# The 16 meta tokens last in a head's output step, and their rows turned by a 16-column product

## The chip, the cores and the metric

One core of a Trainium2 chip runs the whole program. The metric is the time of one execution in microseconds (us). Lower is better. TensorE (PE) does the matrix products, VectorE (DVE) and ScalarE (ACT) the elementwise work and the reading of PSUM, GpSimd (POOL) a few small operations, and SyncE (SP) issues the loads.

## The reference, cut to what matters

Two layers work on 528 tokens: 16 learned meta tokens, prepended, and 512 tokens of input. Each layer has eight heads, four of retention and four of gated linear attention (GLA). A head's output goes through a normalisation over its 128 values and is multiplied with a gate; the eight heads together go through one output projection.

```python
def _head_group_norm(o, w):           # retention heads
    mu = jnp.mean(o, axis=-1, keepdims=True)
    var = jnp.mean(jnp.square(o - mu), axis=-1, keepdims=True)
    y = (o - mu) * lax.rsqrt(var + EPS)
...
def _head_rms_norm(o, w):             # GLA heads
    y = o * lax.rsqrt(jnp.mean(o * o, axis=-1, keepdims=True) + EPS)
...
    o_ret = _head_group_norm(o_ret, ret_norm_w) * jax.nn.silu(rg.astype(jnp.float32))
    o_gla = _head_rms_norm(o_gla, gla_norm_w) * jax.nn.silu(gr.astype(jnp.float32))
    merged = jnp.concatenate([o_ret, o_gla], axis=-1).astype(h.dtype)
    return merged @ w_out
```

The rest of a layer is the input projection (`h @ w_in`, 3600 columns), and a gated MLP with a short convolution.

## The kernel before, in words

Activations lie transposed: features on partitions, the 528 tokens along the free dimension, cut into two column ranges (`SPLIT` at 232). Weights come as float32, and are split into a high and a low float16 part (L122 on ACT, L126 on DVE); each product of a weight tile is three float16 matmuls (L472 to L474). `mixer` walks over the tiles of the input projection (PSUM tile `pj`), and after each it calls `advance`, which takes steps of generators that work on the heads whose inputs are there. After the last tile, `drain` runs what is left of them, and `out_proj` (PSUM tile `po`) follows.

For the heads the tokens are cut differently, in `HEADS`: piece 0 is the 16 meta tokens, pieces 1 to 4 are 128 tokens each. `head_out` is the step at the end of a head. A call takes one retention head or two GLA heads, so a layer has six calls for its eight heads.

- Products. Per head, pieces 1 to 4 go into one PSUM bank `o`, piece 0 into another, `o2`, of which 16 rows are used. L777 makes `o2`, L779 the inner part of the four pieces, L783 adds the part from the state. A float32 product appears as two matmuls in the trace.
- Statistics. For a retention head, L794 and L795 on DVE, per piece; L403 on DVE and a power on POOL (L406) give the reciprocal roots of all five pieces at once. For GLA heads, squares with a sum on ACT (L801), then L405 on DVE and L406.
- Scaling. Each piece is scaled into an SBUF tile: by L806 on DVE (retention) or L808 on ACT (GLA). Pieces 1 to 4 go into `on`, piece 0 into `ont`, a slot of a shared room (the trace calls it `room`) whose unused rows were zeroed.
- A pause of two steps and a wait for the gate; then the turn. L819 transposes each piece back to features on partitions, into PSUM tiles `pto`: one for pieces 0, 1, 2 (272 columns), one for pieces 3, 4 (256 columns). The transpose of piece 0 writes 128 columns, of which those behind the first 16 are written again by piece 1. L822 on DVE multiplies a finished `pto` with norm weight and gate, L410 (ACT) and L411 (DVE) split it to float16 in `merged`.

The list `each` sets the order of the pieces in statistics and scaling: piece 0 first.

PSUM tiles come from two pools: `pmm` with three banks for the large products, `pmx` with five for all else, `o`, `o2` and `pto` among them.

The order in which the instructions stand in each engine's queue is the one of the Python program only up to the ninth weight tile of the first layer (`manual_schedule`). From there on a planner orders each engine's queue when the program is built: it takes the work in the order written, but lets later work pass what by its own reckoning is not ready. On the chip the queues are then fixed: an instruction that waits holds up all behind it on its engine.

Of the kernel before, what the change touches and what calls it, by code (L numbers as in the profile page):

```python
# [14 lines left out]
P = 128  # L15
NMETA = 16
SEQ = 512
L = NMETA + SEQ
# [11 lines left out]
HEADS = [(0, NMETA)] + [(NMETA + P * i, P) for i in range(4)]  # L30
MID = HEADS[3][0]
# [187 lines left out]
class Kern:  # L219
# [547 lines left out]
    def head_out(self, heads):  # L767

        nc = self.nc
        n = len(heads)
        os = [self.mx([P, 4, P], "o") for _ in heads]
        o2s = [self.mx([P, P], "o2") for _ in heads]
        for (intra, _, _, vn, *_), o, o2 in zip(heads, os, o2s):
            nc.tensor.matmul(o2, intra(0), vn(0), start=True, stop=True)  # L777
            for i in range(4):
                nc.tensor.matmul(o[:, i, :], intra(i + 1), vn(i + 1), start=i == 0, stop=i == 0, skip_group_check=i > 0)  # L779
        for i in range(4):  # L780
            c0 = HEADS[i + 1][0]
            for (_, qT, sn, *_), o in zip(heads, os):
                nc.tensor.matmul(o[:, i, :], qT[:, c0 : c0 + P], sn[:, i, :], start=False, stop=True, skip_group_check=True)  # L783
        src = lambda h, i: os[h][:, i - 1, :] if i else o2s[h][:NMETA]
        ret = heads[0][-1] is not None
        onvs = [(self.g([P, 4, P], F32, "on"), self.sm([P, P], "ont")) for _ in heads]
        to = lambda h, i: onvs[h][0][:, i - 1, :] if i else onvs[h][1][:NMETA]
        each = [(h, i, HEADS[i][1]) for h in range(n) for i in range(5)]
        if ret:
            mv = self.sm([P, 5, 2], "mv")  # L790
            nc.gpsimd.memset(mv[:, 0, :], 1.0)
            for h, i, wi in each:
                st = self.sm([P, 6], "bst")
                nc.vector.bn_stats(out=st[:wi], in_=src(h, i))  # L794
                nc.vector.bn_aggr(out=mv[:wi, i, :], in_=st[:wi])  # L795
            r = self.rstd(mv[:, :, 1], 5, 1.0, self.decay[:, 1, heads[0][-1], :])
        else:
            q = self.sm([P, n, 5], "ms")
            nc.gpsimd.memset(q[:, :, 0], 1.0)
            for h, i, wi in each:  # L800
                nc.scalar.activation(to(h, i), src(h, i), AF.Square, accum_out=q[:wi, h, i : i + 1])  # L801
            r = self.rstd(q.rearrange("p h i -> p (h i)"), 5 * n, 1.0 / P, EPS * 64.0)
        for h, i, wi in each:
            rr = r[:wi, 5 * h + i : 5 * h + i + 1]
            if ret:
                nc.vector.tensor_scalar(out=to(h, i), in0=src(h, i), scalar1=mv[:wi, i, 0:1], scalar2=rr, op0=ALU.subtract, op1=ALU.mult)  # L806
            else:
                nc.scalar.activation(to(h, i), src(h, i), AF.Copy, scale=rr)  # L808
        yield
        yield from self.pause(2)  # L810
        for (on, ont), (*_, wcol, gate, slot, _) in zip(onvs, heads):
            while gate[0] is None:
                yield "waits"
            merged = self.merged[slot] = self.g([P, 2, L], F16, "merged")
            for t0, t1, n0, n1 in [(0, 3, 0, MID), (3, 5, MID, L)]:
                pt = self.mx([P, WN], "pto")
                for t in range(t0, t1):
                    c0 = HEADS[t][0] - n0
                    nc.tensor.transpose(pt[:, c0 : c0 + P], on[:, t - 1, :] if t else ont, self.ident)  # L819
                t = self.sm([P, WN], "tmp")  # L820
                w = n1 - n0
                nc.vector.scalar_tensor_tensor(out=t[:, :w], in0=pt[:, :w], scalar=self.par[:, wcol : wcol + 1], in1=gate[0][:, n0:n1],  # L822
                                               op0=ALU.mult, op1=ALU.mult)
                self.split(merged, t[:, :w], n0, n1)
            yield
# [673 lines left out]
```

## Time and profile before

| | before |
|---|---|
| runs | 1238.57 us median of 3 (1238.42 to 1238.85) |
| the profiled execution | 1238.61 us; first to last instruction 1236.8 us |
| granted TensorE clock | 0.997 |
| PE / weight loads / DVE / ACT / POOL busy | 1214.2 / 1015.2 / 871.4 / 676.8 / 162.9 us |
| chain of work that ended last | PE 80%, DVE 10%, ACT 4% |

The "busy" time of an engine counts each instruction from its start to its end, and matmuls overlap; so the distance from one matmul's start to the next start tells more than their durations. In the timeline a row is start, duration, engine, line, operation, tiles out<-in, shape and count, and in brackets the idle time before it with what ended it.

### The profile page before, as it was taken

The page shows a single profiled execution, that of the slowest core. Times are in us where ns is not written, and L with a number is a line of the kernel's source. Part 1 is how long each engine was busy: PE and PEld are TensorE (multiplying, and loading weights), DVE is VectorE, ACT ScalarE, POOL GpSimd, SP SyncE. Part 2 cuts the span into 40 slices and gives each one's busy share as a digit, 9 for nine tenths or more (in the row PEclk, how much of TensorE's full clock was granted, in tenths as well). Part 3 has the DMA queues.
Part 4 walks back from the last instruction along what each step waited for, and adds up shares of the span by engine and source line. Part 5 has one row for each costly group of instructions (what it writes and reads, how often), then busy time and mean ns, then how long its engine had stood idle before and what let it go on. Part 6 is the DMA issues. An engine that isn't in the chain of part 4 may idle for free.

```text
span 1236.8 us, 26441 instructions
## 1 busy us (share of the span) xinstructions
PE 1214.2 (98%) x11031; PEld 1015.2 (82%) x11031; DVE 871.4 (70%) x1541; ACT 676.8 (55%) x1337; POOL 162.9 (13%) x211
## 2 busy tenths in 40 slices
PE   9999999999999999999999999999999999999997
PEld 8778889888788888888887788898798888886444
DVE  5677845367998889623465878443779998887686
ACT  5675444454776666523335754454637776664452
POOL 2012311153000000000230123011520000000001
PEclk9999999999999999999999999999999999999999
DMA  7932221131422423424232332221303363304471
GB/s 199 277 103 86 67 73 52 52 92 46 131 75 69 120 87 108 141 80 102 69 105 68 104 87 70 71 68 52 103 19 103 96 178 104 120 1 171 147 253 68
DMA packets 207259, 124.17 MB, mean 100 GB/s; under 512 B 6992, under 2 KB 194692, under 8 KB 207140
## 3 DMA queue, kind: packets, MB, share of 16 engines
q1 hardware_dynamic: 206836, 121.83, 33.8%
q8 instruction: 86, 1.41, 0.5%
q0 software_dynamic: 160, 0.52, 0.1%
q14 instruction: 33, 0.27, 0.1%
q10 hardware_dynamic: 144, 0.13, 0.0%
HBM read 120.37 MB, written 2.10 MB: 99 GB/s over the span
## 4 chain that ended last, share of the span: by engine, by line
PE 80%; DVE 10%; ACT 4%; issue 3%; POOL 2%; DMA 1%; SPq 0%; POOLq 0%; DVEq 0%; ACTq 0%
PE pl L1340 8%; PE pu L473 8%; PE pu L474 8%; PE pu L472 8%; PE pj L472 7%; PE pj L474 6%; PE pj L473 6%; PE pp L1159 5%; PE pd L472 3%; PE pd L473 3%; PE pd L474 3%; PE po L472 2%; PE po L474 2%; PE po L473 2%; DVE unit L126 2%
## 5 line engine op out<-in xcount | busy, mean ns | idle before, releaser
L473 PE MATMUL pu<-every,unit 128*128 128x296 f16 (+2 forms) x1120 | 306.1, 274 | 2.6 <-DVE every L411 2.6
L474 PE MATMUL pu<-every,unit 128*128 128x296 f16 (+2 forms) x1120 | 306.1, 274 | 0.0
L472 PE MATMUL pu<-every,unit 128*128 128x296 f16 (+2 forms) x1120 | 304.5, 274 | 0.7 <-ACT every L410 0.7
L474 PEld LDWEIGHTS <-unit 128*128 128x128 f16 x2572 | 252.0, 98 | 42.1 <-issue 3.4
L472 PEld LDWEIGHTS <-unit 128*128 128x128 f16 x2572 | 252.2, 98 | 41.1 <-issue 3.1
L473 PEld LDWEIGHTS <-unit 128*128 128x128 f16 x2572 | 252.4, 98 | 39.6 <-issue 2.9
L126 DVE SCALAR_TENSOR_TENSOR unit<-st,unit 128x1024 f16<-128x1024 f32 (+1 forms) x165 | 202.1, 1228 | 78.9 <-ACT unit L122 78.3
L472 PE MATMUL pj<-every,unit 128*128 128x296 f16 (+2 forms) x888 | 244.9, 276 | 3.0 <-ACT gv L1013 1.6
L474 PE MATMUL pj<-every,unit 128*128 128x296 f16 (+2 forms) x888 | 244.7, 276 | 0.9 <-DVE unit L126 0.9
L473 PE MATMUL pj<-every,unit 128*128 128x296 f16 (+2 forms) x888 | 244.9, 276 | 0.0
L122 ACT ACTIVATE unit<-st 128x1024 f16<-128x1024 f32 x163 | 169.7, 1042 | 79.2 <-PE pd L474 22.8
L438 DVE TENSOR_TENSOR acc<-acc,sq 128x296 f32<-128x296 f32 (+2 forms) x60 | 33.3, 556 | 73.9 <-ACT sq L436 72.1
L1159 PEld LDWEIGHTS <-unit 128*128 128x128 f16 x756 | 73.9, 98 | 13.3 <-issue 2.3
L474 PE MATMUL pd<-av,unit 128*128 128x232 f16 (+1 forms) x308 | 84.7, 276 | 0.0
L473 PE MATMUL pd<-av,unit 128*128 128x232 f16 (+1 forms) x308 | 84.7, 276 | 0.0
L472 PE MATMUL pd<-av,unit 128*128 128x296 f16 (+1 forms) x308 | 84.5, 276 | 0.0
L1215 ACT ACTIVATE u<-pu 128x296 f32<-128x296 f32 (+2 forms) x140 | 52.5, 378 | 50.2 <-PE pu L474 49.2
L406 POOL TENSOR_TENSOR every<-every 128x5 f32<-128x5 f32 (+6 forms) x31 | 38.1, 1231 | 293.5 <-DVE every L405 253.3
L1340 PE MATMUL pl<-unit,fk 128*128 128x512 f16 x330 | 71.4, 379 | 0.0
L474 PE MATMUL po<-merged,unit 128*128 128x296 f16 (+2 forms) x256 | 69.6, 274 | 0.0
L473 PE MATMUL po<-merged,unit 128*128 128x296 f16 (+2 forms) x256 | 69.6, 274 | 0.0
L1204 DVE SCALAR_TENSOR_TENSOR cg<-u,every,cg 128x527 f32<-128x527 f32 (+1 forms) x88 | 66.2, 752 | 4.7 <-ACT cg L1199 4.3
(272 smaller groups left out, 1908.6 us busy)
## 6 DMA issues: line engine op xcount, KB each, us to landing
st<-in_ffn_up SPq DMA_DIRECT2D x70, 512.0 KB, 4.0
st<-in_w_in SPq DMA_DIRECT2D x56, 512.0 KB, 4.4
st<-in_ffn_down SPq DMA_DIRECT2D x46, 512.0 KB, 4.4
st<-in_ffn_up SPq DMA_DIRECT2D x36, 256.0 KB, 3.8
st<-in_w_out SPq DMA_DIRECT2D x16, 512.0 KB, 4.2
st<-in_ffn_down SPq DMA_DIRECT2D x8, 384.0 KB, 3.6
out<-yo SPq DMA_DIRECT2D x7, 256.0 KB, 2.1
xt<-in_x SPq DMA_DIRECT2D x6, 256.0 KB, 6.3
```

What stands on the lines that cost most here:

```text
L122: self.kern.nc.scalar.activation(self.u[:, 0], self.st, AF.Copy, scale=SW)
L126: self.kern.nc.vector.scalar_tensor_tensor(out=self.u[:, 1, ks], in0=self.st[:, ks], scalar=SW, in1=self.u[:, 0, ks], op0=ALU.mult, op1=AL ...
L406: nc.gpsimd.tensor_tensor(out=r[:w, :n], in0=t[:w, :n], in1=self.mhalf[:w, :n], op=ALU.pow)
L438: eng.tensor_tensor(out=acc[:, :n], in0=acc[:, :n], in1=sq[:, :n], op=ALU.add)
L472: nc.tensor.matmul(ps[:, :n], w[:, 0, kk, :], x[:, 0, n0:n1], start=first, stop=False)
L473: nc.tensor.matmul(ps[:, :n], w[:, 0, kk, :], x[:, 1, n0:n1], start=False, stop=False)
L474: nc.tensor.matmul(ps[:, :n], w[:, 1, kk, :], x[:, 0, n0:n1], start=False, stop=last)
L1159: mm = lambda p, q, **kw: nc.tensor.matmul(ps, u[:, p, k, :], x[k][:, q], skip_group_check=more, **kw)
L1204: nc.vector.scalar_tensor_tensor(out=to, in0=u[:, max(lo, d) - d : L - d], scalar=self.cvec[:, ci(i) : ci(i) + 1], in1=to, op0=ALU.mult, o ...
L1215: nc.scalar.activation(u[:, n0:n1], ps[:, : n1 - n0], AF.Copy, scale=IXW)
L1340: mm = lambda x, w, **kw: nc.tensor.matmul(ps[:, cols], x, w[:, cols], skip_group_check=more, **kw)
```

## The change

In `head_out`, three lists change their order and one operation is replaced:

- the product of piece 0 (`o2`) is written after all products of the pieces 1 to 4 of the call's heads, no longer first of each head;
- statistics and scaling go over the pieces in the order 1, 2, 3, 4, 0;
- the first turn group is written in the order 1, 2, 0, and piece 0 is turned by an ordinary float32 product of `ont` with the first 16 columns of the identity, which writes 16 columns, in place of a transpose that writes 128.

```diff
         for (intra, _, _, vn, *_), o, o2 in zip(heads, os, o2s):
-            nc.tensor.matmul(o2, intra(0), vn(0), start=True, stop=True)
             for i in range(4):
                 nc.tensor.matmul(o[:, i, :], intra(i + 1), vn(i + 1), ...)
         for i in range(4):
...
                 nc.tensor.matmul(o[:, i, :], qT[:, c0 : c0 + P], sn[:, i, :], start=False, stop=True, ...)
+        for (intra, _, _, vn, *_), o2 in zip(heads, o2s):
+            nc.tensor.matmul(o2, intra(0), vn(0), start=True, stop=True)
...
-        each = [(h, i, HEADS[i][1]) for h in range(n) for i in range(5)]
+        each = [(h, i, HEADS[i][1]) for h in range(n) for i in (1, 2, 3, 4, 0)]
...
-            for t0, t1, n0, n1 in [(0, 3, 0, MID), (3, 5, MID, L)]:
+            for ts, n0, n1 in [((1, 2, 0), 0, MID), ((3, 4), MID, L)]:
                 pt = self.mx([P, WN], "pto")
-                for t in range(t0, t1):
+                for t in ts:
                     c0 = HEADS[t][0] - n0
-                    nc.tensor.transpose(pt[:, c0 : c0 + P], on[:, t - 1, :] if t else ont, self.ident)
+                    if t:
+                        nc.tensor.transpose(pt[:, c0 : c0 + P], on[:, t - 1, :], self.ident)
+                    else:
+                        nc.tensor.matmul(pt[:, :NMETA], ont, self.ident[:, :NMETA], start=True, stop=True)
```

## The prediction, made before the change was run

> **What bounds the kernel now.** First the page, for the engines' load and the chain that ended last; then the list of what PE waited for; then the timeline around the longest of those waits.
>
> ```profile
> span 1236.8 us, 26441 instructions
> PE 1214.2 (98%) x11031; PEld 1015.2 (82%) x11031; DVE 871.4 (70%) x1541; ACT 676.8 (55%) x1337; POOL 162.9 (13%) x211
> PE 80%; DVE 10%; ACT 4%; issue 3%; POOL 2%; DMA 1%; SPq 0%; POOLq 0%; DVEq 0%; ACTq 0%
> ...
> PE pto L819 <- DVE room L806: 4.3, 2, 2.3
> ...
> PE pj L472 <- ACT gv L1013: 1.6, 1, 1.6
> ```
>
> PE is the bound: it is busy nearly all of the span and carries 80% of the chain. So what the change does on another engine costs only if PE comes to wait for it, while a matmul added to PE's queue or taken from it counts whole. PE's idle time is small, and the largest item in it (4.3 us, two times) stands on a line of the change: L819, the turn, waits for L806, the scaling, of `room`, which is the meta piece. This is the place in layer 0, PE first, then DVE and POOL:
>
> ```profile
> 227.10 0.26 PE L474 MATMUL pj<-every,unit 128*128 128x232 f16 x1
> 229.33 0.30 PE L819 MATMUL pto<-every,room 128*128 128x128 f32 x1 [1.97 <-DVE room L806]
> 229.47 0.29 PE L472 MATMUL pj<-every,unit 128*128 128x296 f16 x1
> ...
> 231.99 0.27 PE L819 MATMUL pto<-every,on 128*128 128x128 f32 x1
> 232.10 0.29 PE L474 MATMUL pj<-every,unit 128*128 128x296 f16 x1
> 232.22 0.49 PE L819 MATMUL pto<-every,on 128*128 128x128 f32 x3
> 232.55 0.27 PE L819 MATMUL pto<-every,room 128*128 128x128 f32 x1
> ```
>
> ```profile
> 223.22 0.28 DVE L794 BATCH_NORM_STATS2 room<-o 16x6 f32<-16x128 f32 x1 [1.84 <-PE o L777]
> 223.54 0.17 DVE L795 BATCH_NORM_AGGREGATE room<-room 16x2 f32<-16x6 f32 x1
> 226.15 0.88 DVE L794 BATCH_NORM_STATS2 room<-o 128x6 f32<-128x128 f32 x4
> 226.95 0.36 DVE L795 BATCH_NORM_AGGREGATE room<-room 128x2 f32<-128x6 f32 x4
> 227.34 0.17 DVE L403 TENSOR_TENSOR every<-room,every 128x5 f32<-128x5 f32 x1
> 228.79 0.40 DVE L806 TENSOR_SCALAR room<-o,room,every 16x128 f32<-16x128 f32 x1 [1.28 <-POOL every L406]
> 229.12 1.35 DVE L806 TENSOR_SCALAR on<-o,room,every 128x128 f32<-128x128 f32 x4
> ...
> 227.59 1.17 POOL L406 TENSOR_TENSOR every<-every 128x5 f32<-128x5 f32 x1 [6.21 <-DVE every L403]
> ```
>
> PE's queue has the meta piece's turn behind the last `pj` product of one column range. The piece is scaled at 229.19 (228.79 + 0.40), because the chain statistics, sum, power on POOL (1.17 us), scaling has to run first; all the `pj` products behind that turn stand still. Then PE runs 20 `pj` matmuls (229.47 to 231.99, 0.126 us each) before it turns piece 1, though piece 1 was scaled by 229.51. In layer 1 it is the same, 2.30 us of wait and 19 products between ((846.77 - 844.38) / 0.126):
>
> ```profile
> 844.24 0.30 PE L819 MATMUL pto<-every,room 128*128 128x128 f32 x1 [2.30 <-DVE room L806]
> ...
> 846.77 0.27 PE L819 MATMUL pto<-every,on 128*128 128x128 f32 x1
> ```
>
> So the question is what stands at that place of PE's queue when the meta piece is no longer first.
>
> **The change part by part.**
>
> The turn by a product. Sixteen transposes (two layers, eight heads) go, sixteen float32 products with 16 columns come. Both are in the trace, the product as L844's `rst`:
>
> ```profile
> 205.80 0.27 PE L819 MATMUL pto<-every,room 128*128 128x128 f32 x1
> 205.91 0.60 PE L819 MATMUL pto<-every,on 128*128 128x128 f32 x4
> 206.35 0.29 PE L473 MATMUL pj<-every,unit 128*128 128x296 f16 x1
> ...
> 101.85 0.29 PE L844 MATMUL rst<-rq,rk 128*128 128x16 f32 x2
> 101.99 1.14 PE L844 MATMUL rs<-rq,rk 128*128 128x128 f32 x8
> ...
> 222.80 0.38 PE L777 MATMUL o<-room 128*128 128x128 f32 x2
> 223.02 0.26 PE L472 MATMUL pj<-every,unit 128*128 128x232 f16 x1
> ...
> 137.31 0.46 PE lps L920 x24
> ```
>
> A transpose takes PE from 205.80 to 205.91, 0.11 us. The product is two matmuls, each with a load of 128 weights, and takes 0.14 us (101.85 to 101.99): eight times fewer columns save nothing. That makes 16 x 0.03 = +0.5 us, all on PE. Ends: as dear as a product with 128 columns, 0.22 us (222.80 to 223.02), 16 x 0.11 = +1.8 us; as cheap as two small float16 matmuls of L920 (0.46 / 24 = 0.02 each), 16 x (0.04 - 0.11) = -1.1 us. I take +0.5, since `rst` is the same operation in type, rows and columns.
>
> The Trainium skill, "TensorE: Matmul & The Clock Gate", section "Wait — 56ns, not 53.3ns?", says that start-to-start never drops below about 25 ns however small a matmul is. If that floor were all that is paid, a product would take 50 ns and the sixteen would save about 1 us, an estimate from the page; the `rst` row, at 0.14 us a pair, disagrees as far as weights have to be loaded.
>
> The `o2` product moved. The same 32 matmuls, so nothing for PE itself: 0.22 us where it stands alone between `pj` matmuls. What it moves is PSUM: `o2` is made at 222.80 and the products of `o` start only a microsecond later,
>
> ```profile
> 223.81 1.07 PE L779 MATMUL o<-vn,dgr 128*128 128x128 f32 x8
> ```
>
> which I read as `o` waiting for a free bank that `o2` took first; written the other way round, `o` may start up to 1.0 us earlier. Bounds on the waits of both layers together: -2.0 to 0.
>
> The statistics' and scaling's order. In the retention head the meta piece's L794 and L795 ran at 223.22, three microseconds ahead of the others; now they come last, ahead of L403. One more L794 takes 0.20 us there ((0.88 - 0.28) / 3), one more L795 0.07: the power and the first scaling come up to 0.27 us later, in two places 0 to +0.5 us. Queued behind them on DVE is only the scaling, and who waits for that is the turn. Against the earlier start of `o` I set both together at 0. The first scaling is then piece 1's and the meta piece's the last of five, 4 x 0.32 = 1.3 us later (1.35 for four, less 0.39, by three). In GLA calls the two squares of the meta pieces, made early before, come behind the eight others, 2 x 0.25 us; their cover is that the last call's squares are done 13 us ahead of that call's turn (219.1 against 232.55):
>
> ```profile
> 216.96 0.28 ACT L801 ACTIVATE on<-o 128x128 f32<-128x128 f32 x1 [2.31 <-PE o L783]
> 217.22 0.27 ACT L801 ACTIVATE on<-o 128x128 f32<-128x128 f32 x1
> ...
> 218.88 0.25 ACT L801 ACTIVATION_READ_ACCUMULATOR on<-o 128x1 f32 x1
> ```
>
> If that cover were gone, ACT's L808 would be late next. POOL's memsets and SP's loads are untouched; no DMA is moved.
>
> The first turn. Now piece 1's. My forecast leaves it at the place where the meta piece's turn was: the planner put a turn there for the first piece that is scaled, piece 1 is now that piece, and its scaling starts when the meta piece's did. PE then waits the same 2.0 and 2.3 us, and pieces 2 and 0 come behind `pj` products as pieces 1 and 2 did.
>
> Sum: 1238.61 (the profiled execution; its span of 1236.8 and 1.8 around it; the median of the runs, 1238.57, is the same within 0.04) + 0.5 + 0 + 0 = 1239.1 us, no change that could be told: the runs lie within 0.5 us, but a program planned anew can shift by more than that, so I call only 0.2%, 2.5 us, a difference.
>
> **The rivals.**
>
> The wait goes. If the first turn keeps the place that piece 1's turn has now, 20 products further back, PE reaches it at 227.20 + 20 x 0.126 = 229.7, when piece 1 is scaled (229.2 as the first of the five). Nothing waits, in either layer: 1238.61 - 4.3 + 0.5 = 1234.8 us. For it: piece 1's place has held in both layers to within a few tenths of the moment when that piece would be scaled, so the planner knows that time well, and it is the meta piece's turn that stands too early. The trace doesn't show why it did. Against it: that early place may belong to whichever piece is first.
>
> A longer wait. If the three turns of the first group come together at the early place, PE waits for the last scaling, the meta piece's, instead of the first: 1.28 us longer, and 0.27 for the later statistics, per layer: 1238.61 + 2 x 1.55 + 0.5 = 1242.2 us. It decides when the added wait is over 1.0 us per layer ((2.5 - 0.5) / 2). For it: in the rows at 205.80 all five turns stand side by side. Against it: at the place in question the queue has products between pieces 0 and 1 and between 1 and 2, so there the turns come as the pieces do.
>
> Cheap products. The 16 columns cost only two starts: with the 0.02 us of the L920 row, 1238.61 - 1.1 = 1237.5 us; still no difference that can be told. `rst` speaks against it.
>
> The planner orders all queues behind the first head anew, so waits elsewhere may come or go; the largest of them is the 1.6 us of L1013, so this is worth some 3 us either way.
>
> **How the numbers follow.** The forecast has 0.46, cheap products 0.04, the wait gone 0.30, the longer wait 0.14, and another order elsewhere that decides 0.06, half to each side. Faster by over 0.2%: 0.30 + 0.03 = 0.33; within 0.2%: 0.46 + 0.04 = 0.50; slower: 0.14 + 0.03 = 0.17. The forecast's own range, with the ends of its terms, is 1236.1 to 1241.0: below, cheap products and part of the earlier start (-1.1 - 1.4), above, dear products and the later statistics (+1.8 + 0.5). The whole range goes from 1234.3, the wait gone and the products free, to 1242.2, the longer wait.
>
> **What would show it.** Right: in the list of what PE waited for, L819 still has about 4.3 us in two waits, now for L806 of `on`; the matmuls of the meta turns have 16 columns and stand 0.14 us before the next start; L794's row of 16 partitions comes behind those of 128. The wait gone: L819 has left that list, and the row of the first turn carries no idle time. The longer wait: L819 waits for `room`, over 3 us each time. Wrong altogether: new waits on `pj` or `po` products that the list of before doesn't have, for PSUM or for weights.

## The result, and the profile after

| | time, us (median, lowest to highest) | runs | profiled execution | its span |
|---|---|---|---|---|
| before | 1238.49 (1236.84 to 1238.85) | 6 | 1238.61 | 1236.8 |
| after | 1232.45 (1231.88 to 1234.01) | 6 | 1233.94 | 1232.2 |

The ratio is 0.9955, with a 95% interval of 0.9943 to 0.9968: 6 us, or half a per cent, faster. 1239.1 was forecast, and the time is below the range too (1234.3).

The page of the changed kernel, its load and its chain, and the top of the list of what PE waited for (total, number of times, longest):

```profile
span 1232.2 us, 26476 instructions
PE 1212.6 (98%) x11047; PEld 1014.5 (82%) x11047; DVE 868.8 (71%) x1541; ACT 675.9 (55%) x1337; POOL 161.6 (13%) x211
PE 81%; DVE 10%; ACT 4%; issue 2%; DMA 1%; POOL 1%; SPq 1%; POOLq 0%; DVEq 0%; ACTq 0%
```

```profile
PE pu L473 <- DVE every L411: 2.6, 5, 0.6
PE pj L472 <- ACT gv L1017: 1.6, 1, 1.6
```

PE still bounds the kernel and has 16 matmuls more. The first line of that list before, 4.3 us of the turn waiting for the scaling, is gone, and the two lines that lead the list now were there before. (Further down stands 1.1 us of `pts`, early in layer 0, which the first trace of before lacks and its second trace has too, with 0.9.) The same place in layer 0, PE first (most of the `pj` rows are left out), then DVE, then POOL:

```profile
219.96 1.05 PE L778 MATMUL o<-vn,dgr 128*128 128x128 f32 x8
220.85 1.06 PE L782 MATMUL o<-sn,rq 128*128 128x128 f32 x8
221.74 0.39 PE L784 MATMUL o<-room 128*128 128x128 f32 x2
221.97 0.29 PE L474 MATMUL pj<-every,unit 128*128 128x296 f16 x1
...
227.01 0.26 PE L474 MATMUL pj<-every,unit 128*128 128x232 f16 x1
227.11 0.38 PE L821 MATMUL pto<-every,on 128*128 128x128 f32 x2
227.33 0.29 PE L472 MATMUL pj<-every,unit 128*128 128x296 f16 x1
...
228.59 0.60 PE L821 MATMUL pto<-every,on 128*128 128x128 f32 x4
229.03 0.52 PE L823 MATMUL pto<-every,room 128*128 128x16 f32 x4
```

```profile
222.29 1.07 DVE L795 BATCH_NORM_STATS2 room<-o 128x6 f32<-128x128 f32 x5
...
225.18 1.37 DVE L807 TENSOR_SCALAR on<-o,room,every 128x128 f32<-128x128 f32 x4 [1.28 <-POOL every L406]
226.46 0.39 DVE L807 TENSOR_SCALAR room<-o,room,every 16x128 f32<-16x128 f32 x1
```

```profile
223.98 1.17 POOL L406 TENSOR_TENSOR every<-every 128x5 f32<-128x5 f32 x1 [7.08 <-DVE every L403]
```

Three things are to be seen. The chain of statistics, sum, power and scaling is no shorter: 2.89 us from the first L795 to the first L807, of which POOL takes 1.17; it was 2.64 (226.15 to 228.79), and the 0.25 is the fifth piece. But the products of `o` stand at 219.96 where they stood at 223.81, while the first turn did not move: it stands behind the last `pj` product of the same column range, at 227.11, where PE had come to it at 227.20 and then waited. Counted by the `pj` matmuls of the layer that are still to come, the last product of the call went from 40 to 70 (in layer 1 from 37 to 70), and the first turn stayed at 24 (in layer 1 it went from 23 to 17). So 46 of them lie between the two in layer 0, where there were 16. Piece 1 is scaled at 225.6, 1.5 us before PE asks for it, so no row of the turn carries idle time. And the meta piece is last everywhere, as written: its scaling at 226.46, its product behind the transposes.

Where the time went, from the starts of all of PE's matmuls in the two traces (a matmul has the time until the next one starts), in us per layer (each of the two traces holds one stretch at half clock within `pj`, worth 1.7 us, see below):

| | layer 0 | layer 1 |
|---|---|---|
| `pj` (the wait stood behind these) | 161.07 to 159.08 | 159.77 to 157.37 |
| products of `o` and `o2` | 17.03 to 16.40 | 17.05 to 16.42 |
| the turn's transposes and products | 4.51 to 4.94 | 4.50 to 4.94 |

That is -4.4 for the waits, -1.3 for `o`, +0.9 for the turn: -4.8, against -4.7 between the two profiled executions (1238.61 to 1233.94). The `o` term was in no step of the prediction. It is the call of two heads of the other kind (GLA), here after:

```profile
208.81 1.96 PE L778 MATMUL o<-vn,dg 128*128 128x128 f32 x16
210.70 1.16 PE L782 MATMUL o<-sn,room 64*128 64x128 f32 x16
211.79 0.71 PE L784 MATMUL o<-room 128*128 128x128 f32 x4
```

and the same call before:

```profile
212.97 1.07 PE L779 MATMUL o<-vn,dg 128*128 128x128 f32 x8
213.87 0.39 PE L777 MATMUL o<-room 128*128 128x128 f32 x2
214.19 0.71 PE L783 MATMUL o<-sn,room 64*128 64x128 f32 x4
214.82 1.16 PE L779 MATMUL o<-vn,dg 128*128 128x128 f32 x8
215.91 1.16 PE L783 MATMUL o<-sn,room 64*128 64x128 f32 x12
```

Before, PE did one head's 128-row products, four of the 64-row products, then went back. After, it does all 128-row products, then all sixteen 64-row ones, and these sixteen take the 1.16 us that twelve took; the 0.63 us of the four by themselves (214.19 to 214.82) are gone.

### The profile page after: what moved, and what is told of

Same layout as the page of the kernel before. It is cut to its first block, busy times and chain, and to the rows that moved or that the text cites. A ratio compares the mean times of both kernels' runs of the same rounds, so it can differ in the third digit from the quotient of the medians.

```text
span 1232.2 us, 26476 instructions
## 1 busy us (share of the span) xinstructions
PE 1212.6 (98%) x11047; PEld 1014.5 (82%) x11047; DVE 868.8 (71%) x1541; ACT 675.9 (55%) x1337; POOL 161.6 (13%) x211
## 4 chain that ended last, share of the span: by engine, by line
PE 81%; DVE 10%; ACT 4%; issue 2%; DMA 1%; POOL 1%; SPq 1%; POOLq 0%; DVEq 0%; ACTq 0%
PE pl L1344 8%; PE pu L473 8%; PE pu L474 8%; PE pu L472 8%; PE pj L472 7%; PE pj L474 7%; PE pj L473 7%; PE pp L1163 5%; PE pd L472 3%; PE pd L474 3%; PE pd L473 3%; PE po L472 2%; PE po L474 2%; PE po L473 2%; DVE unit L126 2%
```

## The experiments

Two theories stood after the result. **The bank:** `o2`, made first, holds one of the PSUM banks that the pools share, `o` waits in the plan for the next to come free, and everything behind it in the planned queue hangs on when `o` is done; the moved product frees that. (The pools do share: in the programs as they were built, tiles of `pmm` and of `pmx` lie in any of eight banks, not in three and five of their own.) **The piece:** the bank is a side matter; a turn that starts with the meta piece is put too early, and starting with piece 1 (in the lists or in the turn) puts it later. The counts of `pj` matmuls still to come tell the two apart: by the first theory the products come forward, by the second the turn goes back. First each part by itself, three rounds each on one chip with 27 runs of before (median 1239.05).

**Only the product of `o2` last:**

```
-            nc.tensor.matmul(o2, intra(0), vn(0), start=True, stop=True)   # ahead of o's products
...
+        for (intra, _, _, vn, *_), o2 in zip(heads, o2s):                  # behind them all
+            nc.tensor.matmul(o2, intra(0), vn(0), start=True, stop=True)
```

> Only the product of the meta piece is moved behind the others; lists and turn are those of before. Theory A (with the product out of the way, the products of the pieces 1 to 4 start earlier, the chain of statistics, power and scaling is over before PE comes to the turn, and the wait goes by that alone): L819 gone from PE's waits in both layers (-4.4 us), some 50 projection matmuls in PE's queue between the last retention head's products and its first turn instead of 16, the products of o 0.5 us a layer cheaper as in the changed kernel: 1238.5 - 4.4 - 1.2 = about 1233 us, 0.9955. Theory B (the wait belongs to the meta piece being first in the turn, and goes only where that is undone): the wait stays, 1237 to 1238.5 us, 0.999 to 1.000.

Measured: 1233.71 us, ratio 0.9964 (0.9952 to 0.9977). No turn is in the list of PE's waits. This part alone takes the waits away, with the meta piece still first in the lists and in the turn. It is the products that came forward: 87 and 86 `pj` matmuls (layer 0 and 1) are still to come behind them, where it was 40 and 37, and the turn stands a little earlier too, at 31 and 28. The cheaper `o` that I expected did not come: 17.1 us a layer, no less than before.

**Only the lists:**

```
-        each = [(h, i, HEADS[i][1]) for h in range(n) for i in range(5)]
+        each = [(h, i, HEADS[i][1]) for h in range(n) for i in (1, 2, 3, 4, 0)]
```

> Only the list of statistics and scaling has the meta piece last; products and turn are those of before. Theory A: the products of o start no earlier, so the wait stays at 2.0 and 2.3 us, and it may grow by up to 0.3 each for the later statistics: 1238.5 to 1239.1 us. Theory B: the meta piece is still first in the turn, wait stays too, 1238.5. Theory C (the planner puts a turn where it reckons the scaled piece to be ready, and it reckons only the early-scaled meta piece too early): with the meta piece scaled last its turn moves back behind a whole column range, and the wait goes: 1238.5 - 4.4 = 1234.1 us.

Measured: 1234.57 us, ratio 0.9969 (0.9960 to 0.9979). What is left of the turn's waits, and where `o` stands:

```profile
PE pto L819 <- DVE room L806: 0.4, 1, 0.4
```

```profile
223.15 0.38 PE L777 MATMUL o<-room 128*128 128x128 f32 x2
...
224.75 1.07 PE L779 MATMUL o<-vn,dgr 128*128 128x128 f32 x8
```

`o` is not earlier here (224.75): `o2` stands ahead of it with fourteen `pj` matmuls between. It is the turn that went back, behind 34 `pj` matmuls and so behind the last of the layer, which is the third theory of the expectation. So the wait can be closed from either end, and the lists do it from the other end than the product.

**Only the turn, product first in its group** (the order 0, 1, 2 kept), and **only the turn, product last** (1, 2, 0):

```
...
-                for t in range(t0, t1):
+                for t in ts:                      # (0, 1, 2) or (1, 2, 0), then (3, 4)
...
-                    nc.tensor.transpose(pt[:, c0 : c0 + P], on[:, t - 1, :] if t else ont, self.ident)
+                    if t:
+                        nc.tensor.transpose(pt[:, c0 : c0 + P], on[:, t - 1, :], self.ident)
+                    else:
+                        nc.tensor.matmul(pt[:, :NMETA], ont, self.ident[:, :NMETA], start=True, stop=True)
```

> Only the transpose of the meta piece becomes a product with 16 columns, in the old order 0, 1, 2; all else as before. By every theory the first turn stays at its early place and the wait at about 2.0 and 2.3 us; so this prices the product: the prediction's 0.03 us each gives +0.5 us; the changed kernel's trace, where the turns together took 0.44 us a layer more, gives +0.9 us. 1239.0 to 1239.4 us.

> Only the turn is changed, to a product that comes after the pieces 1 and 2; products and lists as before. The recorded forecast (piece 1 takes the early place): the wait stays, 1239 us. Its rival and theory B (the first turn stands where piece 1's turn stood before, some 37 projection matmuls behind the products of o): the wait goes, 1238.5 - 4.4 + 0.9 = 1235.0 us. Theory A alone: the wait stays, since the products of o start no earlier.

Measured: first, 1239.58 us, ratio 1.0005 (0.9996 to 1.0014), with waits of 1.86 and 2.09 us still there; last, 1235.81 us, ratio 0.9983 (0.9973 to 0.9992). The product by itself brings nothing; its place does. With the product last, the turn goes back in both layers (3 `pj` matmuls are still to come behind it, and 40 and 38 behind the products, as before); layer 1's wait is gone, but layer 0's only went to another instruction. In the list of waits and in the timeline of that kernel:

```profile
PE pj L472 <- DVE room L806: 1.8, 1, 1.8
```

```profile
227.65 0.26 PE L474 MATMUL pj<-every,unit 128*128 128x232 f16 x1
229.75 0.30 PE L472 MATMUL pj<-every,unit 128*128 128x296 f16 x1 [1.85 <-DVE room L806]
```

A projection's product has no use for the scaled meta piece. What it needs and that scaling gives up is the PSUM that `o2` occupied: in the program as built, this `pj` tile lies in the bank of the `o2` that the scaling reads. This row is the plainest sign that the bank of `o2` is what PE's queue can stand on.

**The bank by itself.** Everything in the order of before, meta piece first, transposes; only the `o2` of a call's heads lie in one bank together:

```
-        o2s = [self.mx([P, P], "o2") for _ in heads]
+        o2 = self.mx([P, n, P], "o2")
+        o2s = [o2[:, h, :] for h in range(n)]
```

> Products, lists and turn stand as before, the meta piece first everywhere; only the o2 tiles of a call's heads share one PSUM bank, so a GLA call holds three banks and not four. Theory A, sharpened (the last retention head's products come late because no PSUM bank is free for o, and that lateness makes the wait): PE's queue has about 59 projection matmuls between these products and the first turn instead of 16, and the wait of L819 goes in both layers though the meta piece is still scaled and turned first: 1238.5 - 4.4 = 1234.1 us. Theory B (the order of the pieces makes the wait): it stays, 1238.5 us.

Measured (five rounds, 13 runs of before, median 1238.84): 1234.36 us, the median of five executions without a sixth of 2549.76 us; ratio 0.9965 (0.9953 to 0.9978). No turn is in the list of waits. PE, then DVE:

```profile
217.77 0.38 PE L778 MATMUL o<-room 128*128 128x128 f32 x2
...
218.12 1.05 PE L780 MATMUL o<-vn,dgr 128*128 128x128 f32 x8
219.01 1.06 PE L784 MATMUL o<-sn,rq 128*128 128x128 f32 x8
...
226.39 0.27 PE L820 MATMUL pto<-every,room 128*128 128x128 f32 x1
```

```profile
223.90 0.40 DVE L807 TENSOR_SCALAR room<-o,room,every 16x128 f32<-16x128 f32 x1 [1.28 <-POOL every L406]
```

The product of `o2` is still first here, and `o` follows it by 0.35 us, where it was 1.0 before. The meta piece, still scaled first and turned first, is ready at 224.3, 2.1 us ahead of its turn. So one bank less is enough, and no order of pieces has to change: the theory of the bank holds. The products came forward (96 `pj` matmuls still to come in each layer), and the turn with them (37 and 45).

Which bank it is needs care. This kernel differs only in the calls of two heads, which hold three banks instead of four; the last retention head still takes two. So a bank that the GLA call ahead of it holds is enough to set the place of that head's products; the order of `o2` and `o` within the head need not change. The program of before as built says the same: the last head's `o` is put into the bank that the first `o2` of that GLA call leaves when ACT has scaled it. On the chip this was done at 221.78:

```profile
221.42 0.36 ACT L808 ACTIVATE room<-o,every 16x128 f32<-16x128 f32 x1 [0.50 <-POOL every L406]
```

PE came to `o` at 223.81, 2.0 us later and without idle time. So `o` was not held up by the bank while the kernel ran; it stands late in an order that was made when the program was built, by the planner's own reckoning of when a bank comes free.

The theory of the piece is not refuted as a second way, since the lists alone did it. But it is not what the changed kernel does: there the turn kept its place in layer 0, and in layer 1 it gave 6 of the 39 `pj` matmuls that came in between (53 where there were 14); the products gave the rest.

**The change less one part.** Without the turn's part, without the moved product, and (later, with 9 runs of before, median 1238.58) without the lists:

> The changed kernel with the old turn: five transposes, piece 0 first; products and lists as changed. Theory A: no wait, and the turns cheaper than the product's: by the prediction's 0.03 us each 0.5 us below the changed kernel, by its trace (0.44 us a layer) 0.9 us below. Theory B: the wait comes back, 4 us above the changed kernel.

> The changed kernel with the old place of the product: the meta piece's product first, lists and turn as changed. Theory A: the last head's products are as late as before; 10 matmuls of 232 columns and 16 of 296 (3.0 us) stand between them and the first turn, which the chain needs some 3.8 us for: waits of 0.7 to 0.9 us in each layer are left, 1238.5 - 4.4 + 1.6 + 0.9 = 1236.6 us. Theory B: no wait at all, 1235.0 us.

> The product of `o2` last and the turn by a product, the lists in the old order. Theory of the bank: as with the moved product alone no turn waits (5.3 us gained in that run), and the turn's product adds up to 0.9 us: 1233.7 to 1234.6 us. Rival, each of the three parts brings a share of its own: without the lists it loses what the lists alone gained (4.5 us) against the changed kernel: 1236 to 1238 us.

> The changed kernel again, beside the other three on the same chip, to compare them with: every theory, 0.9955 of before as measured, or -4.8 us if only what its trace accounts for in the heads' stages is counted.

| kernel | us | ratio (95%) | `pj`, both layers | `o`, `o2` | turn |
|---|---|---|---|---|---|
| changed, beside the first two | 1233.22 | 0.9954 (0.9942 to 0.9967) | 315.9 | 32.8 | 9.9 |
| less the turn's part | 1233.33 | 0.9955 (0.9941 to 0.9968) | 316.4 | 33.0 | 8.8 |
| less the moved product | 1235.80 | 0.9974 (0.9964 to 0.9984) | 316.5 | 34.2 | 10.4 |
| less the lists | 1235.02 | 0.9967 (0.9955 to 0.9980) | 314.3 | 34.5 | 9.8 |

The last three columns are from the starts of PE's matmuls, as above, in the profiled executions; all but the last row hold one stretch at half clock, worth 1.7 us (below). The moved product is worth the most, as 2.6 us are lost without it (1235.80 less 1233.22); without the lists it is 1.6 us (1235.02 less 1233.46, the changed kernel beside it, below). The kernel without the moved product has hardly a wait left, so what I expected of waits there, 0.7 to 0.9 us each, was a miss. It loses 1.4 us in `o`, 0.6 in `pj` and 0.6 in the turn, whose transposes are held up a little in layer 0. Without the turn's part the turn is 1.0 us cheaper; 0.7 of that went in `pj` and `o` of that execution, and the time is the same, not the 0.5 to 0.9 us less that I expected. Without the lists the kernel gets no wait either, but loses the 0.8 us per layer in `o`; its 1235.02 lies between the two theories' figures, and neither had this term. Its GLA call:

```profile
207.66 1.05 PE L778 MATMUL o<-vn,dg 128*128 128x128 f32 x8
208.64 0.71 PE L782 MATMUL o<-sn,room 64*128 64x128 f32 x4
209.28 1.16 PE L778 MATMUL o<-vn,dg 128*128 128x128 f32 x8
210.37 1.16 PE L782 MATMUL o<-sn,room 64*128 64x128 f32 x12
211.45 0.71 PE L784 MATMUL o<-room 128*128 128x128 f32 x4
```

From 207.66 to 211.45 are 3.79 us for what took 2.98 in the changed kernel (208.81 to 211.79). The head-by-head order shows in every kernel that lacks one of the two, moved product and lists; the sixteen-by-sixteen order in each that has both, by the time of `o` (at least 17.0 us in a layer, or 16.4 to 16.5). Why the planner needs both for it, the traces don't show.

**Both ways together, without the dear turn:** the product and the lists as changed, transposes as before, one bank for the `o2` of a call (it is the `o2` that share it, not the products with the state that the expectation names); with the changed kernel beside it once more.

> Products and lists with the meta piece last as in the changed kernel, the turn a transpose and first as before, and the products of one call's heads with the state in one PSUM bank together. Theory of the bank (a product of the meta piece that holds a bank delays the next head's products, and the order of all that follows hangs on that) with the turn's price as the traces gave it (0.055 us more for a product with 16 columns than for a transpose, 16 of them, 0.9 us): no wait of a turn, `o` products 0.6 us cheaper per layer as in the changed kernel, and no 0.9 us for the turn: 1232.3 to 1232.9 us, that is up to 0.9 below the changed kernel. Rival: one bank for two heads gives nothing more once the product stands last, and the turn's price is paid back elsewhere: the same as the changed kernel within 0.4 us, 1232.8 to 1233.6.

> The changed kernel once more, on the same chip as the others of this call: 0.995 to 0.996 of before, 1232.5 to 1233.5 us, no wait of a turn. For the half-clock stretch: if it belongs to a fixed place, 655 to 665 us shows a clock of 0.83 as in both earlier traces of this kernel; if it falls after one wait or another by chance, it may stand elsewhere or be absent.

Measured: 1233.36 us (1233.22 to 1233.75), ratio 0.9958 (0.9944 to 0.9971); the changed kernel beside it 1233.46 (1232.28 to 1234.01), 0.9957 (0.9944 to 0.9969). In the rows the turn is 0.51 us cheaper in each layer (4.94 to 4.43), as expected, but the time isn't: the profiled execution has a stretch at half clock, which that of the changed kernel beside it lacks. So this version does not beat the changed kernel by anything that can be told, and the 1232.3 to 1232.9 of the bank's theory was a miss; whether it would in executions without the stretch stays open, for its five runs lie within 0.6 us of one another.

**The clock.** Some executions hold a stretch of 3.4 us in which PE runs at half clock. Two theories: a fixed place in the program, or chance after one wait or another.

> The kernel before once more, one look at its clock. Theory of chance (a stretch of 3.4 us at half clock falls after one wait of PE or another, and not at one place): the stretch is absent at 655 to 665 us, or stands after another wait, among them those of the turns at 229 and 844 us. Rival, a fixed place: 655 to 665 us shows 0.83 as in the first trace. The waits of the turns are 4.3 us in two places either way.

Measured: 1238.83 us; the stretch was behind the turn's wait in layer 1. Windows of 10 us (busy time of PE, its loads, DVE, ACT and POOL with counts; the granted clock; DMA). Of before, the first trace:

```profile
655.00:665.00 10.00, 8.47 (x57) 6.03 (x55) 7.30 (x18) 4.27 (x11) 0.00 (x0) 0.83 0.01 2
```

Of before, the second trace, and its PE rows in that place:

```profile
655.00:665.00 10.00, 8.47 (x70) 6.61 (x68) 7.31 (x18) 4.26 (x11) 0.00 (x0) 1.00 0.01 2
840.00:850.00 10.00, 7.72 (x55) 6.01 (x54) 4.94 (x19) 1.75 (x4) 1.27 (x3) 0.83 0.19 54
```

```profile
842.87 0.45 PE L819 MATMUL pto<-every,room 128*128 128x128 f32 x1 [2.28 <-DVE room L806]
843.11 0.45 PE L473 MATMUL pj<-every,unit 128*128 128x296 f16 x1
...
846.25 0.29 PE L474 MATMUL pj<-every,unit 128*128 128x296 f16 x1
```

Right behind the wait of 2.28 us a `pj` matmul takes 0.247 us (843.11 to 843.35 to 843.60) instead of 0.126, until 846.2. The same kernel had it from 659.4 in the other trace: chance, not one place. The changed kernel had it in two of its three traces, both from 657.4; the third has full clock there, and ran 1232.28 instead of 1233.94: 1.7 us, which is half of 3.4. The turn's wait was one of the places where it can fall, so I take it, without a run that shows it, that a wait removed saves more, on average, than its length.

## Why the prediction was wrong

**The earlier start of `o`** is the term that failed. I let `o` start up to 1.0 us earlier, bounded that at -2.0 to 0 us for the waits of both layers, and then set it against the later statistics at 0. `o` started 3.85 us earlier in layer 0 (223.81 to 219.96), and the waits went whole: -4.4 us where the sum had 0. The moved product alone bore it out, with 5.3 us by the medians of its experiment (1239.05 to 1233.71), 4.5 by its ratio.

The reading that `o` waits for a bank that `o2` took first was right of the plan, as the shared bank and the program as built show; but it was the plan alone that waited, for on the chip the bank was free 2.0 us before. The size was wrong because the bound was the gap of 1.0 us in the old order, and such a gap says nothing about the order that a planner makes without its cause. Most of the 3.85 us was gained ahead of that gap: the retention call before starts 2.7 us earlier already (203.12 to 200.45), and the GLA call between them 4.2 us (212.97 to 208.81).

**The first turn.** That it stays "at the place where the meta piece's turn was" held: in layer 0 it stands behind the same `pj` product as before, at 227.11. What did not hold is the half sentence behind it, "its scaling starts when the meta piece's did": it starts at 225.18 where that one started at 228.79. With the scaling 3.6 us earlier at an unmoved turn there is no wait of 2.0 us.

The rival "the wait goes" gave 1234.8, and the sign I had named for it, L819 out of the list and no idle time in the turn's first row, is what the profile shows. That its figure came near is luck in part: it had the turn 20 products further back and the scaling where it was, and what happened is the reverse. The lists and the turn alone do move the turn back, as it said, but the changed kernel does not. The range's upper end, by the way, adds up to 1240.9 and not 1241.0, on which nothing hangs.

**The turn by a product.** 0.03 us each was forecast, +0.5 in all; measured +0.43 and +0.44 per layer, 0.055 each, +0.9 in all. The product's own two matmuls are as I had them, 0.14 us (231.62 to 231.76 below). The other half falls on the transpose behind it (0.14 us to the next start where it was 0.11), as I read it because the matmul of 16 columns is too short to cover the next load of weights; no run takes the two apart. The changed kernel's rows, loads by line (ns: least, median, most), then PE:

```profile
L821 PEld LDWEIGHTS pto<-every,on x64: 138/141/225, 185.4 to 844.9; 128*128 128x128 f32 x64
L823 PEld LDWEIGHTS pto<-every,room x32: 190/192/192, 185.6 to 843.8; 128*128 128x128 f32 x32
```

```profile
231.41 0.38 PE L821 MATMUL pto<-every,on 128*128 128x128 f32 x2
231.62 0.29 PE L823 MATMUL pto<-every,room 128*128 128x16 f32 x2
231.76 0.26 PE L472 MATMUL po<-merged,unit 128*128 128x232 f16 x1
```

Two loads of 0.19 us stand for each product (x32 for sixteen), one of 0.14 for a transpose. The rival "cheap products" is out. So is, for this product, the 50 ns that I had estimated from the Trainium skill ("TensorE: Matmul & The Clock Gate", section "Wait — 56ns, not 53.3ns?"): the trace has 0.14 us.

**The statistics' and scaling's order.** The five statistics do come in one run, and the meta piece's scaling is last, at 226.46. The first scaling is 0.25 us later in its chain, as worked out (0.27); nothing of it is on PE's path, since piece 1 has 1.5 us to spare. The GLA squares stayed hidden, as forecast: no wait of the turn for ACT is in the list.

**Not in the prediction:** `o` itself, -1.3 us. I had written "nothing for PE itself" for the moved product, and counted matmuls without asking in what order the two heads' come. "Another order elsewhere" had a chance of 0.06 and no term.

Sum with the measured terms: 1238.61 - 4.4 - 1.3 + 0.9 = 1233.8, and the profiled execution took 1233.94. The median moved by more (6.0 us), because three of the six runs of the changed kernel lay near 1232, as those without the half-clock stretch do. From the lowest of all runs of before to the lowest of all after, 1236.68 to 1231.88, it is 4.8 us, as in the rows.

## What to carry to other kernels

A small tile that takes a whole PSUM bank costs what its bank costs, and the sign of it can stand on an instruction that has nothing to do with it: look whom the last reader of that tile releases. Where queues are planned when the program is built, look for the cause of a late instruction in the plan too: it can stand late without ever waiting on the chip. There, a part that frees a bank or a dependency moves everything behind it, so its price is not bounded by the gap seen in the old order; give it the largest wait downstream as its bound, and a chance to match. When a wait goes, see which of its two ends moved, by counting what lies between and what is still to come. A product with few columns in place of a transpose saves nothing where weights must be loaded: here it cost 0.055 us more, half of it on the next matmul.

## What was not expected of the hardware

The half-clock stretch in the midst of a kernel in which PE is busy 98% of the span. In each of the eleven traces that have it, it starts within 1.3 us behind a wait of PE. Some of these waits are of about 2 us, as the 2.28 us above; in the run with only the turn's product, first, it came 0.8 us behind a wait of 1.86 us:

```profile
229.80 0.37 PE L822 MATMUL pto<-every,room 128*128 128x16 f32 x2 [1.86 <-DVE room L806]
...
230.64 0.35 PE L474 MATMUL pj<-every,unit 128*128 128x296 f16 x1
230.78 0.45 PE L472 MATMUL pj<-every,unit 128*128 128x296 f16 x1
```

But a wait need not be so long. In the first trace of before, two of the changed kernel, and two more, it starts behind waits of 0.87 and 0.65 us, here in the changed kernel:

```profile
655.99 0.29 PE L730 MATMUL pj<-every,unit 128*128 128x296 f16 x1 [0.87 <-ACT every L410]
...
657.18 0.64 PE L730 MATMUL pj<-every,unit 128*128 128x296 f16 x2 [0.65 <-DVE every L411]
657.61 0.45 PE L473 MATMUL pj<-every,unit 128*128 128x296 f16 x1
```

The Trainium skill, "TensorE: Matmul & The Clock Gate", section "What's actually happening", tells of a window of 3413 ns that runs free of the kernel, over which PE's activity sets full or half clock. The length seen here, from 842.9 to 846.2, and the chance from run to run agree with that. Its section "HAM oscillation — how this bites in real kernels" puts the harm at gaps of over 3.4 us; here waits of 0.65 to 2.28 us had a stretch behind them, at 1.7 us each. What decides whether one comes, no run shows. It also shows in the times: 27 runs of before on one chip fall into eight from 1236.7 to 1237.5, seven from 1238.5 to 1239.2 and twelve from 1239.8 to 1240.6, in steps of about 1.6 us; all sixteen runs of the changed kernel lie from 1231.9 to 1234.0. That these levels are no, one and two such stretches is a guess: the two traces of before are both of the second level and hold one each, and the mean granted clock of the runs falls with the levels (0.998, then 0.997 to 0.998, then 0.995 to 0.997), but no trace was taken of a run of before at the first level or the third.
